# W1 chunks and W2 pairs in turn: both halves of W2 by seven products, with the sums carried by ScalarE

## The chip, the cores and the metric

The kernel runs on one core of one Trainium2 chip. The metric is the device time of one execution in microseconds (us). TensorE (PE) multiplies matrices, VectorE (DVE) and ScalarE (ACT) do the elementwise work, SyncE (SP) issues nearly all loads. PSUM has eight banks, each of which holds one sum of 128 x 512 fp32 values.

## The reference

Two layers over 256 positions of width 2048; the change touches the MLP alone, which stands once in each layer:

```python
def sq_relu_mlp(x, w1, w2):
    return jnp.square(jax.nn.relu(x @ w1)) @ w2        # w1 2048 x 8192, w2 8192 x 2048

for layer in range(2):
    mix = short_conv_mixer(...) if layer == 0 else mla_mixer(...)
    h = layer_norm(ALPHA * h + mix, ...)
    h = layer_norm(ALPHA * h + sq_relu_mlp(h, w1[layer], w2[layer]), ...)
```

## The kernel before

**Two parts for each number.** Every fp32 operand is split into a high part, rounded for the matmul (`hi`, made by ScalarE), and a low part, what is left (`lo`, made by VectorE); `split` does that (lines 120 to 123). A product is three matmuls: high by high, high by low, low by high (`dot`, lines 271 to 275). For W1 the high weights take both parts of x at once, 512 columns wide (`high`, line 201), and the low weights take x's high part, 256 columns (`low`, line 205).

**Weights.** `stream` lists all weights in the order of their use, in units of 128 x 1024 values (512 KB). `prepare` loads a unit into one of five buffers (`raws`) and splits it into one of eight pairs of buffers (`whl`). `take` hands the next units to a product and prepares ahead of it, up to `LOOK` = 5 units. The order of instructions on each engine is fixed when the program is built, by a scheduler that follows the order of the code for the most part; every engine works through its own list in order.

**The MLP.** `mlp` goes over the 8192 hidden columns in eight eighths (`q`). For each it makes eight chunks of 128 hidden columns (`products`, one chunk is 16 high and 16 low matmuls over 16 K tiles, in turn), evacuates each with ScalarE and VectorE (`whole`), applies Relu and Square, and splits the result. Then it multiplies the eighth by its rows of W2. Two chunks of hidden columns, 256 rows of W2, make a pair. The 2048 output columns are four blocks of 512, for two blocks of 128 tokens.

**Seven products.** A pair times two blocks of output columns, for both token blocks, is a 2 x 2 by 2 x 2 product of blocks: eight block products, or seven by Winograd's scheme, for which sums and differences of the blocks are needed. For the hidden values these are S1 to S4 (lines 604 to 607, VectorE); for the weights T1 to T4 (`prepare`, lines 163 to 176, VectorE too, and their splits). Before, the first two of four output blocks go by seven products in the eighths named in `FAST`, 1 to 6 in layer 0 and 1 to 7 in layer 1 (`down_fast`, seven banks at once; `combine` adds them into `acc`). The rest goes block by block with eight (`down`, `down_late`), and VectorE adds every result into `acc`, which is in SBUF.

**Ends.** The first eighth is done against x that is not normalized yet (`mm_wide`), while `normal` normalizes x. In layer 0 the last eighth is interleaved with transposes for the next layer (`to_wide`), in layer 1 with the last norm and the output (`to_out`).

Of the kernel before, what the change touches and what calls it, by code (L numbers as in the profile page):

```python
# [31 lines left out]
LOOK = 5  # L32
# [3 lines left out]
FAST = {0: range(1, NQ - 1), 1: range(1, NQ)}  # L36
FIRST = ((0, 2, 4, 8), (0, 4, 8))
GROUP = 3
# [4 lines left out]
LAG = 16  # L43
# [4 lines left out]
def trunk(ctx: ExitStack, tc: tile.TileContext, xT, vecs, w_in, w_out, w_kv, w_q, w_uk, w_uv,  # L48
# [12 lines left out]
    ROOM = {"a1": 16896, "a2": 16896, "b": 33280, "c": 16384}  # L61
# [8 lines left out]
    def halves(w):  # L70

        lead = len(w.shape) - 2
        return [(w,)] if lead == 0 else [h for i in range(w.shape[0]) for h in halves(w[i])]
# [5 lines left out]

    def mlp_stream(l):  # L80
        out = []
        for q in range(NQ):
            out += halves(w1[l, q * QC:(q + 1) * QC])
            lead = 0
            if q in FAST[l]:
                out += [(w2f[l, q, j, 0], w2f[l, q, j, 1]) for j in range(QC // 2)]
                lead = 2
            out += halves(w2[l, q, lead:])
        return out
# [4 lines left out]
    stream += halves(w_o) + mlp_stream(1)  # L94

    class Banks:


        more, count = None, 0
# [12 lines left out]
        @classmethod  # L112
        def next(cls):
            cls.count += 1
            return cls.more if cls.more is not None and cls.count % 8 >= 4 else pmm

    state = {"split": 0, "next": 0}
# [13 lines left out]
    def load(i, raw, cuts):  # L131

        hi, lo = ready[i] = parts(i)
        for b0, b1 in zip(cuts, cuts[1:]):
            at, cols = slice(b0, b1), slice(P * b0, P * b1)
            nc.sync.dma_start(raw[:, cols], stream[i][0][:, cols])
            yield
            split(hi[:, at, :], lo[:, at, :], tiled(raw[:, cols]))
            yield
# [6 lines left out]
    def prepare(i):  # L146

        if len(stream[i]) == 1:
            raw = load_raw(i, stream[i][0])
            hi, lo = ready[i] = parts(i)  # L150
            split(hi, lo, tiled(raw))
            return
        r1, r2 = (load_raw(f"{i}_{j}", src) for j, src in enumerate(stream[i]))
        out = []

        def finished(r, name):
            hi, lo = parts(name)
            split(hi, lo, tiled(r))
            out.append((hi, lo))

        b22, (b21, b12) = r1[:, BW:], (r2[:, :BW], r2[:, BW:])
        finished(r1, f"{i}_1")
# [4 lines left out]
        finished(t, f"{i}_t")  # L167
        nc.vector.tensor_tensor(b12, b22, t[:, :BW], ALU.subtract)
        finished(r2, f"{i}_2")
        t4 = r1[:, :BW]  # L170
        nc.vector.tensor_tensor(t4, b21, b12, ALU.subtract)
        f = state["fast"].tile([P, 2, BW], F32R, tag="t4", name=f"t4_{i}")
        split(f[:, 0, :], f[:, 1, :], t4)
        b1, t13, b2 = ([[v.rearrange("p b c -> p (b c)")[:, o:o + BW] for v in w] for o in (0, BW)] for w in out)
        ready[i] = {"11": b1[0], "22": b1[1], "21": b2[0], "T2": b2[1], "T1": t13[0], "T3": t13[1],
                    "T4": [f[:, 0, :], f[:, 1, :]]}

    def size(i):

        return 1 if len(stream[i]) == 1 else 3  # L180

    def take(halves=2):

        i = state["next"]
        state["next"] += halves
        ahead = -sum(size(j) for j in range(i, i + halves))
        for j in range(i, len(stream)):
            ahead += size(j)
            if ahead > LOOK:
                break  # L190
            if j >= state["split"]:
                prepare(j)
                state["split"] = j + 1
        return [ready.pop(i + j) for j in range(halves)]
# [12 lines left out]
    def mm_run(wps, x, k0, k1, nk, tiles_first=False, turn=None):  # L207
# [4 lines left out]
        for k, (w, ps) in order:  # L212
            if k == turn:
                low(ps, w, k, x[k], False)
                high(ps, w, k, x[k], False)
                continue
            high(ps, w, k, x[k], k == 0)
            low(ps, w, k, x[k], k == nk - 1)

    def mm_lag(ps, w, x):  # L220

        for k in range(NC + LAG):
            if k < NC:
                high(ps, w, k, x[k], k == 0)
            if k >= LAG:
                low(ps, w, k - LAG, x[k - LAG], k == NC + LAG - 1)

# [25 lines left out]
    def products(n, x, group=0, cuts=(), turn=None, lag=True):  # L253
# [7 lines left out]
        for i in range(group, n):  # L261
            w = take()
            ps = psum("ps_u")
            if lag:
                mm_lag(ps, w, x)
            else:
                mm_run([(w, ps)], x, 0, NC, NC, turn=turn if i == 0 else None)
# [3 lines left out]
    def dot(ps, w, x, first, last):  # L271

        nc.tensor.matmul(ps, x[0], w[0], start=first, stop=False)  # L273
        nc.tensor.matmul(ps, x[0], w[1], start=False, stop=False)  # L274
        nc.tensor.matmul(ps, x[1], w[0], start=False, stop=last)  # L275
# [34 lines left out]

    FACTORS = (("4", "22", "T4"), ("2", "12", "21"), ("3", "S4", "22"), ("1", "11", "11"),
               ("6", "S2", "T2"), ("7", "S3", "T3"), ("5", "S1", "T1"))

    def down_fast(x, forms):

        ps = {p: psum(f"ps_f{p}") for p, _, _ in FACTORS}
        n = len(x) // 2
        for j in range(n):
            b, = take(1)
            a = {"11": held(x[2 * j], 0), "12": held(x[2 * j + 1], 0), "22": held(x[2 * j + 1], 1)}  # L320
            for i in range(4):
                a[f"S{i + 1}"] = [v[:, j, (4 + i) * P:(5 + i) * P] for v in forms]
            for p, l, r in FACTORS:
                dot(ps[p], b[r], a[l], j == 0, j == n - 1)
        return ps
# [191 lines left out]
    state["split"] = 2 * GROUP  # L517
# [32 lines left out]
    def mlp(idx, ln, begin, blocks, fast):  # L550
# [12 lines left out]

        def block(n, t):
            return acc[:, t, n * BW:(n + 1) * BW]

        def put(n, t, ps):
            if q == 0:
                nc.scalar.copy(block(n, t), ps)
                for _ in range(2):  # L570
                    normal()
            else:
                nc.vector.tensor_tensor(block(n, t), block(n, t), ps, ALU.add)

        for q in range(NQ):
            forms = [array(a, F32R, f"h{idx}_{q}_{a}", QC // 2, 8 * P) for a in ("c", "a2")] if q else None
            if q == NQ - 1:
                begin(block)
            if forms is None:
                ht = array("c", F32R, f"h{idx}_{q}", QC, 2 * T)  # L580
                h = [ht[:, k, :] for k in range(QC)]
            else:
                h = [tuple(v[:, k // 2, (k % 2) * T:(k % 2 + 1) * T] for v in forms) for k in range(QC)]

            def hidden(m, ps, evac, *func):
                if forms is None:
                    f = tmp.tile([P, T], F32, tag="fh", name="fh", bufs=3)
                else:
                    if m % 2 == 0:
                        state["pair"] = fast.tile([P, 8 * P], F32, tag="sf", name="sf")  # L590
                    f = state["pair"][:, m % 2 * T:(m % 2 + 1) * T]
                evac(ps, f, *func)
                if not func:
                    nc.scalar.activation(f, f, AF.Relu)  # L594
                nc.scalar.activation(f, f, AF.Square)
                if forms is None:
                    put_split(h[m], f)
                elif m % 2:
                    hi, lo = (v[:, m // 2, :] for v in forms)
                    src, cols = state["pair"], 4 * P  # L600
                    if q in FAST[idx // 2]:
                        cols = 8 * P
                        a11, a21, a12, a22, s1, s2, s3, s4 = (src[:, i * P:(i + 1) * P] for i in range(8))
                        nc.vector.tensor_tensor(s1, a21, a22, ALU.add)
                        nc.vector.tensor_tensor(s3, a21, a11, ALU.subtract)
                        nc.vector.tensor_tensor(s2, s1, a11, ALU.subtract)
                        nc.vector.tensor_tensor(s4, a12, s2, ALU.subtract)
                    split(hi[:, :cols], lo[:, :cols], src[:, :cols])

            if q == 0:  # L610
                for m in range(QC):
                    if m < GROUP:
                        if m == 0:
                            ws = ln.ws if ln.ws else group_of(GROUP)
                            if not ln.ws:
                                mm_wide(ws, ln.xd)
                            ln.finish()
# [6 lines left out]
                    if m > 0:  # L624
                        normal()
# [393 lines left out]
```

## Time and profile before

| | us |
|---|---|
| median of three runs | 2032.91 (2032.8 to 2034.95) |
| the profiled execution | 2034.58 |
| its span, first to last instruction | 2032.5 |
| TensorE busy | 2013.5 (99%) |
| weight loads of TensorE | 1760.0 (87%) |
| VectorE busy | 1654.6 (81%) |
| ScalarE busy | 1181.9 (58%) |
| read from HBM | 381.25 MB, 189 GB/s over the span |

The granted clock of TensorE is 0.996 over the span. A busy time is the time in which the engine has something in work, so operations that overlap at their ends count once; the mean duration of one operation in a group is longer than the distance from its start to the next one's. In the names, PE is TensorE, PEld its weight loads, SPq the queue of SyncE.

### The profile page before, as it was taken

The page shows a single profiled execution, that of the slowest core. Times are in us where ns is not written, and L with a number is a line of the kernel's source. Part 1 is how long each engine was busy: PE and PEld are TensorE (multiplying, and loading weights), DVE is VectorE, ACT ScalarE, POOL GpSimd, SP SyncE. Part 2 cuts the span into 40 slices and gives each one's busy share as a digit, 9 for nine tenths or more (in the row PEclk, how much of TensorE's full clock was granted, in tenths as well). Part 3 has the DMA queues.
Part 4 walks back from the last instruction along what each step waited for, and adds up shares of the span by engine and source line. Part 5 has one row for each costly group of instructions (what it writes and reads, how often), then busy time and mean ns, then how long its engine had stood idle before and what let it go on. Part 6 is the DMA issues. An engine that isn't in the chain of part 4 may idle for free.

```text
span 2032.5 us, 30055 instructions
## 1 busy us (share of the span) xinstructions
PE 2013.5 (99%) x11208; PEld 1760.0 (87%) x11208; DVE 1654.6 (81%) x2494; ACT 1181.9 (58%) x1752; POOL 2.3 (0%) x21
## 2 busy tenths in 40 slices
PE   9999999999999999999999999999999999999997
PEld 7888888988888888888889998898888888888885
DVE  7667667677898988989688888777889898898988
ACT  6444445576565565655556655467656566565652
POOL 0000000000000000000000000000000000000000
PEclk9999999999999999999999999999999999999998
DMA  8666656564746557475754534656475665746644
GB/s 297 204 190 189 191 189 190 166 202 139 254 145 227 181 182 254 145 233 174 230 176 149 176 122 134 199 171 201 137 248 152 221 210 161 250 145 224 206 164 152
DMA packets 108002, 385.31 MB, mean 190 GB/s; under 512 B 11984, under 2 KB 13392, under 8 KB 107856
## 3 DMA queue, kind: packets, MB, share of 16 engines
q1 hardware_dynamic: 107712, 383.13, 58.8%
q8 instruction: 88, 1.44, 0.3%
q14 instruction: 58, 0.48, 0.1%
q10 hardware_dynamic: 144, 0.26, 0.0%
HBM read 381.25 MB, written 2.10 MB: 189 GB/s over the span
## 4 chain that ended last, share of the span: by engine, by line
PE 96%; DVE 2%; DMA 1%; issue 1%; ACT 0%; DVEq 0%; ACTq 0%
PE ps_u L201 32%; PE ps_u L205 17%; PE ps_d L273 7%; PE ps_d L274 7%; PE ps_d L275 7%; PE ps_f L274 4%; PE ps_f L275 4%; PE ps_f L273 4%; PE ps_w L247 1%; PE ps_w L245 1%; PE ps_w L246 1%; PE ps_g L247 1%; PE ps_g L245 1%; PE ps_g L246 1%; DMA raw<-in_w2f_dram 1%
## 5 line engine op out<-in xcount | busy, mean ns | idle before, releaser
L123 DVE TENSOR_TENSOR lo<-raw,hi 128x1024 fp32r<-128x1024 f32 x712 | 856.9, 1221 | 257.7 <-ACT hi L122 179.9
L122 ACT CAST hi<-raw 128x1024 fp32r<-128x1024 f32 x712 | 743.6, 1051 | 486.4 <-PE ps_u L201 268.9
L201 PE MATMUL ps_u<-xhl,hi 128*128 128x512 f32 x1792 | 622.1, 392 | 0.0
L205 PE MATMUL ps_u<-xhl,lo 128*128 128x256 f32 x1792 | 499.6, 280 | 0.0
L201 PEld LDWEIGHTS ps_u<-xhl,hi 128*128 128x128 f32 x1792 | 334.4, 187 | 73.1
L205 PEld LDWEIGHTS ps_u<-xhl,lo 128*128 128x128 f32 x1792 | 338.6, 189 | 1.7
L273 PE MATMUL ps_d<-hi,h_c 128*128 128x512 f32 x480 | 186.8, 389 | 0.0
L275 PE MATMUL ps_d<-hi,h_a 128*128 128x512 f32 x480 | 186.6, 389 | 0.0
L274 PE MATMUL ps_d<-lo,h_c 128*128 128x512 f32 x480 | 186.6, 389 | 0.0
L201 PE MATMUL ps_u<-xhl_a,hi 128*128 128x512 f32 x720 | 171.9, 391 | 0.0
L201 PEld LDWEIGHTS ps_u<-xhl_a,hi 128*128 128x128 f32 x720 | 132.4, 188 | 25.7
L274 PEld LDWEIGHTS ps_d<-lo,h_c 128*128 128x128 f32 x480 | 90.1, 188 | 18.8 <-DVE lo L123 0.2
L275 PEld LDWEIGHTS ps_d<-hi,h_a 128*128 128x128 f32 x480 | 90.1, 188 | 18.7
L273 PEld LDWEIGHTS ps_d<-hi,h_c 128*128 128x128 f32 x480 | 90.1, 188 | 18.6
L205 PEld LDWEIGHTS ps_u<-xhl_a,lo 128*128 128x128 f32 x720 | 92.3, 191 | 3.5
L594 ACT ACTIVATE sf<-sf 128x256 f32<-128x256 f32 x112 | 46.7, 417 | 82.1 <-DVE sf L331 81.9
L205 PE MATMUL ps_u<-xhl_a,lo 128*128 128x256 f32 x720 | 93.4, 283 | 0.0
L122 ACT CAST hi_t<-raw_t 128x1024 fp32r<-128x1024 f32 x52 | 54.6, 1050 | 47.1 <-DVE raw_t L165 32.0
L330 ACT COPY t<-ps_u 128x256 f32<-128x256 f32 x157 | 57.0, 363 | 42.1 <-PE ps_u L205 42.1
L274 PE MATMUL ps_f<-lo,h_c 128*128 128x512 f32 x208 | 81.2, 390 | 0.2 <-DVE lo L123 0.2
L275 PE MATMUL ps_f<-hi,h_a 128*128 128x512 f32 x208 | 81.1, 390 | 0.0
L273 PE MATMUL ps_f<-hi,h_c 128*128 128x512 f32 x208 | 80.7, 389 | 0.0
(235 smaller groups left out, 3290.8 us busy)
## 6 DMA issues: line engine op xcount, KB each, us to landing
raw<-in_w_dram SPq DMA_DIRECT2D x408, 512.0 KB, 4.4
raw<-in_w2f_dram SPq DMA_DIRECT2D x104, 512.0 KB, 3.6
raw<-in_w_in_dram SPq DMA_DIRECT2D x90, 512.0 KB, 4.2
raw<-in_w_out_dram SPq DMA_DIRECT2D x32, 512.0 KB, 4.0
raw<-in_w_o_dram SPq DMA_DIRECT2D x32, 512.0 KB, 4.1
raw<-in_w_kv_dram SPq DMA_DIRECT2D x10, 512.0 KB, 4.2
raw<-in_w_q_dram SPq DMA_DIRECT2D x8, 512.0 KB, 4.4
raw<-in_w_uk_dram SPq DMA_DIRECT2D x8, 512.0 KB, 4.5
```

Source lines behind the costliest of these rows:

```text
L122: nc.scalar.copy(hi, src)
L123: nc.vector.tensor_tensor(lo, src, hi.bitcast(F32), ALU.subtract)
L201: nc.tensor.matmul(ps, w[blk // 8][0][:, blk % 8, :], x, start=first, stop=False)
L205: nc.tensor.matmul(ps[:, :T], w[blk // 8][1][:, blk % 8, :], x[:, :T], start=False, stop=last)
L245: nc.tensor.matmul(ps[:, :W], hi, x[k][:, :W], start=k == 0, stop=False)
L246: nc.tensor.matmul(ps[:, :W], lo, x[k][:, :W], start=False, stop=False)
L247: nc.tensor.matmul(ps[:, :W], hi, x[k][:, W:], start=False, stop=k == NC - 1)
L273: nc.tensor.matmul(ps, x[0], w[0], start=first, stop=False)
L274: nc.tensor.matmul(ps, x[0], w[1], start=False, stop=False)
L275: nc.tensor.matmul(ps, x[1], w[0], start=False, stop=last)
L330: nc.scalar.copy(t, ps[:, T:])
L594: nc.scalar.activation(f, f, AF.Relu)
```

## The change

- A plan (`plan`) replaces the eighths. After the first eighth (eight chunks, as before), one group, which is one pair of K tiles of W2 times one half (two blocks) of the output columns, and one chunk of W1 stand in turn. Pairs 0 to 27 of 32 are done so. The halves take turns: two groups of the first half, four of the second, four of the first, and so on. The first three groups follow each other, and three chunks are left over at the end. There are 56 groups and 56 chunks in each layer.
- In both halves every pair of these goes by seven products but the first two (`PLAIN`, eight products). The last four pairs of W2 go block by block with eight products, in both layers.
- The seven sums stay in seven banks over a run of groups. When the half changes (`turn`), ScalarE copies each sum out to SBUF (`spill`) and the other half's sum back into its bank (`seed`), 14 copies; the matmuls then go on adding. Before the last blocks, VectorE adds up the sums of the second half (`fold`) and those of the first (`combine`). The adds into `acc` after every eighth are gone.
- While the sums hold their banks, chunks of W1 have one bank. A chunk does eight high and then eight low matmuls for each of its two units (`mm_like`). Elsewhere `mm_lag` becomes `mm_like`, in the same order.
- `take` prepares by steps, eight units in all from the one in use on; a group by seven products counts three. T4 and the tiles of the forms have two buffers each. S2 and S3 come from one operation.
- The calls that prepare the next norm are spread over the groups in layer 0 (`prepare_one`); in layer 1 the residual is turned before the last blocks rather than before the last eighth.

The diff, cut to its core:

```diff
-LOOK = 5
 RAW, WA = 5, 8
-FAST = {0: range(1, NQ - 1), 1: range(1, NQ)}
+PAIRS = FF // (2 * P)
+KEPT = PAIRS - QC // 2
+SLOTS = 10
+PLAIN = ((0, 1), (0, 1))
...
+    def plan():
+        nxt, b, steps, m, count = [0, 0], 0, [], QC, 0
+        while min(nxt) < KEPT:
+            end = min(nxt[b] + (4 if nxt != [0, 0] else 2), KEPT)
+            run = [(b, j, j in PLAIN[b]) for j in range(nxt[b], end)]
+            for i, (b, j, plain) in enumerate(run):
+                steps.append(("group", b, j, plain, i == 0, i == len(run) - 1))
+                if count >= 3 and m < FF // P:
+                    steps.append(("m", m))
+                    m += 1
+                count += 1
+            nxt[b], b = end, 1 - b
+        return steps + [("m", i) for i in range(m, FF // P)]
...
     def prepare(i):
...
         t = raws.tile([P, 1024], F32, tag="raw", name=f"raw{i}_t")
         two = "p (a c) -> p a c"
         nc.vector.tensor_tensor(t.rearrange(two, a=2), b12.unsqueeze(1).to_broadcast([P, 2, BW]),
                                 r1.rearrange(two, a=2), ALU.subtract)
-        finished(t, f"{i}_t")
         nc.vector.tensor_tensor(b12, b22, t[:, :BW], ALU.subtract)
-        finished(r2, f"{i}_2")
...
+        out["11"], out["22"] = finished(r1, 1)
+        nc.vector.tensor_tensor(b11, b21, b12, ALU.subtract)
+        yield
+        out["T1"], out["T3"] = finished(t, "t")
+        yield
+        out["21"], out["T2"] = finished(r2, 2)
+        f = state["fast"].tile([P, 2, BW], F32R, tag="t4", name=f"t4_{i}", bufs=2)
+        split(f[:, 0, :], f[:, 1, :], b11)
...
+    def take(n=2):
+        i = state["next"]
+        state["next"] += n
+        while state["made"] < min(start[i] + WA, start[-1]):
+            next(making)
+            state["made"] += 1
...
+    def mm_like(ps, w, x, n=NC):
+        for h in range(0, NC, n):
+            for k in range(h, h + n):
+                high(ps, w, k, x[k], k == 0)
+            for k in range(h, h + n):
+                low(ps, w, k, x[k], k == NC - 1)
...
+    FAST = (("1", "11", "11"), ("3", "S4", "22"), ("7", "S3", "T3"), ("5", "S1", "T1"),
+            ("2", "12", "21"), ("6", "S2", "T2"), ("4", "22", "T4"))
...
+        def spill(self, p):
+            if p in self.live:
+                nc.scalar.copy(self.slot(self.live.pop(p)), self.bank[p])
+
+        def seed(self, p, key):
+            if key in self.store:
+                nc.scalar.copy(self.bank[p], self.at(key))
+                self.drop(key)
+                self.live[p] = key
...
+        def turn(self, b, plain):
+            for p, _, _ in FAST:
+                if p in self.bank:
+                    self.spill(p)
+                    self.seed(p, (b, "C" if p == "1" and plain else p))
...
+        sums = Sums(idx)
+        Banks.only = Banks.more
+        count = 0
+        for at, step in enumerate(steps):
+            if step[0] == "m":
+                m = step[1]
+                w, ps = take(), psum("ps_m")
+                mm_like(ps, w, xhl, 8)
+                if m % 2 == 0:
+                    f = pair()
+                half = f[:, m % 2 * T:(m % 2 + 1) * T]
+                whole(ps, half)
+                if m % 2:
+                    nc.scalar.activation(f[:, :4 * P], f[:, :4 * P], AF.Relu)
+                    square(f)
+                    j, cols = m // 2, 4 * P
+                    if j < KEPT:
+                        forms(f)
+                        cols = 8 * P
+                    split(one[:, j % 4, :cols], two[:, j % 4, :cols], f[:, :cols])
+                if m == FF // P - 3:
+                    Banks.only = None
+                continue
+            _, b, j, plain, first, last = step
+            w, = take(1)
...
+            sums.group(b, w, parts_of(j), plain, last, turns)
+            if later:
+                if last:
+                    sums.turn(later[0][1], later[0][3])
...
+            if first and j + 4 >= KEPT and b == 0 and j + 2 >= KEPT:
+                folded = sums.fold(1)
+            if not later:
+                folded = sums.combine(0) + folded
+            if count < 4:
+                normal()
+                normal()
...
-        combine(put, down_fast(h, forms))
         for n in range(2):
+            down(h, put, n)
             for t in range(2):
                 counted(n, t)
         down_late(h, finished, range(2, NB))
```

More of the change, by code (lines that the diff above doesn't have):

```diff
@@ L42 @@
 COL = 128
-LAG = 16
 C_G, C_B, C_CW, C_QG, C_KG, C_END = 0, 64, 128, 176, 180, 184
@@ L94, in trunk @@
     stream += halves(w_o) + mlp_stream(1)
+    size = {"unit": 1, "plain": 2, "fast": 3}
+    start = [0]
+    for kind, *_ in stream:
+        start.append(start[-1] + size[kind])
     class Banks:
-        more, count = None, 0
+        more, count, only = None, 0, None
         @classmethod
@@ L114, in next @@
             cls.count += 1
+            if cls.only is not None:
+                return cls.only
             return cls.more if cls.more is not None and cls.count % 8 >= 4 else pmm
-    state = {"split": 0, "next": 0}
+    state = {"made": 0, "next": 0}
     ready = {}
@@ L251, in group_of, with products @@
         return [(take(), psum("ps_g")) for _ in range(n)]
-    def products(n, x, group=0, cuts=(), turn=None, lag=True):
+    def products(n, x, group=0, cuts=()):
         ws = group_of(group)
@@ L564, in block @@
         def block(n, t):
[L565 removed]
+            return folded[n][t]
         def put(n, t, ps):
[L568 to L617, printed above, removed]
[L618 to L637 removed]
@@ L639, in combine @@
[L639 to L655 removed]
+            nc.vector.tensor_tensor(block(n, t), block(n, t), ps, ALU.add)
@@ L657, in turned, with to_wide @@
+        h = [(one[:, k // 2, k % 2 * T:(k % 2 + 1) * T], two[:, k // 2, k % 2 * T:(k % 2 + 1) * T]) for k in range(QC)]
+        blocks(block, put, h)
+    def to_wide(block, put, h):
         def turned(n):
```

277 lines of the change are left out of this document (163 added, 114 removed).

## The prediction, made before the changed kernel ran

> **What bounds the kernel now.** I read the page first: busy times, the slices, the chain that ended last.
>
> ```profile
> span 2032.5 us, 30055 instructions
> PE 2013.5 (99%) x11208; PEld 1760.0 (87%) x11208; DVE 1654.6 (81%) x2494; ACT 1181.9 (58%) x1752; POOL 2.3 (0%) x21
> PE   9999999999999999999999999999999999999997
> DVE  7667667677898988989688888777889898898988
> PE 96%; DVE 2%; DMA 1%; issue 1%; ACT 0%; DVEq 0%; ACTq 0%
> ```
>
> TensorE is busy in every slice and makes 96% of the chain. Busy matmuls are not yet matmuls at full rate, so I took start times from the timeline of PE, once inside a W2 block and once in the W1 chunk behind it:
>
> ```profile
> 699.67 0.39 PE L274 MATMUL ps_d<-lo,h_c 128*128 128x512 f32 x1
> 714.17 0.39 PE L275 MATMUL ps_d<-hi,h_a 128*128 128x512 f32 x1
> 714.40 0.39 PE L201 MATMUL ps_u<-xhl,hi 128*128 128x512 f32 x1
> 714.63 0.28 PE L205 MATMUL ps_u<-xhl,lo 128*128 128x256 f32 x1
> 719.97 0.39 PE L201 MATMUL ps_u<-xhl,hi 128*128 128x512 f32 x1
> 27.39 3.67 PE ps_u L201 x16
> 31.06 1.91 PE ps_u L205 x16
> 32.97 3.65 PE ps_u L201 x16
> ```
>
> From 699.67 to 714.17 there are 64 steps of one 128x512 matmul: 0.2266 us each. A W1 chunk of 16 high and 16 low matmuls, alternating, takes 719.97 - 714.40 = 5.57 us. The last three rows are from the chain in order of time, an early stage that does its 16 highs first and then its 16 lows: 32.97 - 27.39 = 5.58 us. The order of highs and lows is worth nothing.
>
> So TensorE issues without holes and its matmul count sets the time. VectorE, which makes every low part, is at 81%, and 8 or 9 tenths in most slices of the MLPs. Its rows, from the timeline:
>
> ```profile
> 560.34 0.28 DVE L604 TENSOR_TENSOR sf<-sf 128x128 f32<-128x128 f32 x1
> 560.66 0.29 DVE L606 TENSOR_TENSOR sf<-sf 128x128 f32<-128x128 f32 x1
> 574.86 0.68 DVE L123 TENSOR_TENSOR t<-raw,t 128x512 fp32r<-128x512 f32 x1
> 575.46 1.22 DVE L165 TENSOR_TENSOR raw_t<-raw,raw 128x1024 f32<-128x1024 f32 x1
> 576.60 1.22 DVE L123 TENSOR_TENSOR lo<-raw,hi 128x1024 fp32r<-128x1024 f32 x1
> 577.73 0.29 DVE L605 TENSOR_TENSOR sf<-sf 128x128 f32<-128x128 f32 x1
> 577.94 0.69 DVE L168 TENSOR_TENSOR raw<-raw,raw_t 128x512 f32<-128x512 f32 x1
> 578.54 1.22 DVE L123 TENSOR_TENSOR lo<-raw,hi 128x1024 fp32r<-128x1024 f32 x1
> 579.68 0.42 DVE L331 TENSOR_TENSOR sf<-ps_u,t 128x256 f32<-128x256 f32 x1
> 580.01 0.69 DVE L171 TENSOR_TENSOR raw<-raw 128x512 f32<-128x512 f32 x1
> ```
>
> Start to start: 1.13 us for 1024 columns (576.60 to 577.73), 0.60 for 512 (577.94 to 578.54), 0.33 for 256, 0.21 for 128. One that reads what the one before wrote starts some 0.1 us later (560.34 to 560.66 instead of 0.21).
>
> **What goes: matmuls.** A pair by seven products takes 21 matmuls instead of 24. Before, 13 eighths x 4 pairs x one half = 52 pair-halves go so; after, 26 pairs x 2 halves x 2 layers = 104. That is 52 x 3 = 156 matmuls of 128x512 fewer (the built order of the changed kernel has 5928 instead of 6084; all other shapes keep their counts). 156 x 0.2266 = **-35.4 us**, all on the path. W2 is still loaded once, so SyncE's queue carries as many transfers.
>
> **What comes: VectorE's share of each step.** After the start, a step is one group (4.76 us on TensorE: 21 x 0.2266) and one W1 chunk (5.57): 10.33 us. VectorE has in it, for the group: t and three low parts of 1024 columns (4 x 1.13), two differences and T4's low part of 512 (3 x 0.60); for the chunk: two low parts (2.27) and the evacuation (0.33); in every second step also the forms and the pair's low part (0.21 + 0.33 + 0.21 + 1.13 = 1.88). Sum 8.92 us, or 10.80 with the pair's part, mean **9.86** of 10.33: 95%. Before, the same work stood against down blocks that ask little of VectorE; now 52 such steps follow each other in each layer. The adds into acc (VectorE, 512 columns) go, and none stands in this ledger.
>
> **The loop through the raw buffers.** A share of 95% is safe only if VectorE need not wait. There are five raw buffers, and a step takes five (r1, r2, t and two of W1). The built addresses show that the next group's r1 takes the buffer that t leaves, so its load is issued when t's low part is done. From there to the next group's t low part, in the built order of VectorE: load, ScalarE's high part, then on VectorE low part of r1, t, evacuation, two differences, low part of t.
>
> ```profile
> raw<-in_w2f_dram SPq DMA_DIRECT2D x104, 512.0 KB, 3.6
> DMA to landing us min/median/max: 3.4/4.1/6.6
> 580.46 1.03 ACT L122 CAST hi_t<-raw_t 128x1024 fp32r<-128x1024 f32 x1
> 581.52 1.23 DVE L123 TENSOR_TENSOR lo_t<-raw_t,hi_t 128x1024 fp32r<-128x1024 f32 x1 [0.83 <-ACT hi_t L122]
> core 0: us, PE busy (x) PEld busy (x) DVE busy (x) ACT busy (x) POOL busy (x), PEclk, DMA share, GB/s
> 564.66:602.45 37.79, 37.79 (x201) 32.55 (x200) 36.21 (x52) 26.02 (x39) 0.00 (x0) 1.00 0.40 124
> ```
>
> A load of this tensor lands after 3.6 us (median, page); all raw loads between 560 and 700 us after 3.4 to 6.6, median 4.1. After the change r1 is issued alone and r2 follows 1.13 us later, between the two cases: I take 3.8. High part 1.05; three hand-overs at 0.03 (580.46 + 1.03 to 581.52) make 0.1; VectorE 1.13 + 1.13 + 0.33 + 0.60 + 0.70 + 1.23 = 5.12. The loop is 10.07 us, and in every second step the pair's low part (1.13) stands inside it: 11.20. Mean **10.63**, 0.30 over TensorE's 10.33. 104 steps: **+31 us**. Bounds: at 3.4 us mean 10.23, TensorE paces, 0; at 4.6, mean 11.43, +114. The last row is a stretch of 37.79 us before the change with four group preparations in it (its columns are named in the row above it): VectorE busy 36.21, 96%, TensorE never idle. 9.86 / 0.96 = 10.3 speaks for the lower half, so I stay well below the middle.
>
> **The turns.** After every four groups ScalarE copies seven sums out of PSUM and seven back, 14 copies:
>
> ```profile
> L646 ACT COPY vu<-ps_f 128x512 f32<-128x512 f32 x13 | 7.6, 587 | 38.2 <-DVE acc L573 38.2
> L122 ACT CAST t<-raw 128x512 fp32r<-128x512 f32 x52 | 32.1, 618 | 4.1 <-DVE raw L171 2.9
> L330 ACT COPY t<-ps_u 128x256 f32<-128x256 f32 x157 | 57.0, 363 | 42.1 <-PE ps_u L205 42.1
> L468 ACT ACTIVATE xres<-nu,vec 128x256 f32<-128x256 f32 x48 | 28.5, 598 | 3.9 <-DVE nu L467 3.5
> L594 ACT ACTIVATE sf<-sf 128x256 f32<-128x256 f32 x112 | 46.7, 417 | 82.1 <-DVE sf L331 81.9
> 597.98 1.05 ACT L122 CAST h_c<-sf 128x1024 fp32r<-128x1024 f32 x1
> 598.93 1.05 ACT L122 CAST hi<-raw 128x1024 fp32r<-128x1024 f32 x1
> ```
>
> Out of PSUM is 0.587 us; into PSUM the trace does not show, between 0.417 (256 columns) and 0.618 (512, SBUF to SBUF); I take 0.59, nearest in size: 8.2 us. The Trainium skill (ScalarE: Activation LUTs, Step-by-step) says that ScalarE reaches PSUM faster than SBUF; by that the seven copies back cost somewhat less, and no row here shows it. Queued with the copies in the built order are ten casts of 1024 columns (0.95 start to start), two of 512, an evacuation, Relu and Square (512 columns, 0.62 by the nearest row): 9.5 + 1.2 + 0.4 + 1.2, some 12 us. So the last sum is back 20.2 us after the first left, while TensorE wants it after 4.08 + 5.57 + 4.08 = 13.7 us. The built order of TensorE pulls 6 matmuls of the group after next (1.4 us) and 13 highs and 8 lows of the chunk between (3.9 us) ahead into this hole; 20.2 - 13.7 - 5.3 = 1.2 us are left. In the same two steps TensorE waits 0.6 us for VectorE by the loop above, which covers that much: **0.6 us a turn**, and 24 full turns make **+14 us**. Bounds: 0 where VectorE's waits cover all; 1.6 a turn, +38, if nothing is covered and each copy takes 0.62. A gain is excluded, since nothing goes that ScalarE did in TensorE's way.
>
> **Edits with little behind them.** While the seven sums hold their banks, W1 has one bank: its evacuation (0.36 and 0.42 us) has the next group's 4.76 us to finish in. Normalization: eight of sixteen now stand beside the first plain groups (4 x 5.44 us), three operations of 256 columns on VectorE (1.0 us) and two of 0.60 on ScalarE each, 8 us and 9.6 us in 21.8; the first switch of halves has no chunk between. The fold and the last combine (16 adds of 0.60) stand beside three chunks. I put them together at +4 (0 to 10, the upper end being half of those 9.6 us in each layer). Highs before lows: 0, as above. The residual's transposes move before the last blocks: the same 32, TensorE does them either way.
>
> **Sum.** The profiled execution took 2034.58 us, 2.1 over its span; the median of the three runs, 2032.91, is 1.7 below it. 2034.6 - 35.4 + 31 + 14 + 4 = 2048.2; as a median **2047 us**. A measurement can tell 0.2% (4 us) from no change.
>
> **Rivals.** (a) *TensorE keeps the pace*: loads land at 3.4 us, VectorE's loop is 10.23, and VectorE catches up at each turn. For it: the 96% stretch, in which TensorE did not wait. Against: there it had stored work and only four groups. 2032.9 - 35.4 + 10 to 24 = 2008 to 2022, say **2015**: faster. It decides at a landing time of 3.5 us. (b) *ScalarE's turns alone*: no raw-buffer wait, but 1.6 us a turn: 2032.9 - 35.4 + 38 + 4 = **2040**. (c) *Transfers jam*: four loads of 512 KB within 5 us of each step land at 4.6 us or later: 2047 + 83 = **2130**; the 6.6 in the row above is for it, the page's 3.6 against. (d) *VectorE's operations do not overlap*: by whole durations (1.22, 0.69, 0.42, 0.29) the ledger is 6.95 for the group, 2.86 for the chunk and 1.11 for half a pair, 10.92 us a step, 0.59 over TensorE (61 us in 104), and with turns and edges 2032.9 - 35.4 + 61 + 18 = **2077**; the start times above (1.13 for 1.22) speak against it. The Trainium skill (VectorE: DVE Perf Modes, The DRAIN you can't avoid) says that the next operation does not start until the pipe has emptied; the trace disagrees for these operations. That the matmuls do not go is excluded by the built order.
>
> **Chances.** Forecast 0.52, (a) 0.27, (b) 0.10, (c) 0.08, (d) 0.03. Faster by over 0.2%: nearly all of (a), and 0.03 of the forecast's low end: 0.29. Within 0.2%: 0.02 of (a), 0.04 of the forecast, 0.03 of (b): 0.09. Slower: 0.62. Range 2008 to 2108: it leaves out some of (a) below, most of (c) and the forecast's upper end above. The forecast alone is 2028 to 2108.
>
> **What would show it.** Right: in the steady steps, low part of r1 waits for its high part and that for the load by 0.5 to 1 us, evacuations lag the chunk by several us, PE has small holes of 0.3 us a step and 0.6 more at each turn, VectorE near 93% over these stretches. Wrong: PE dense between turns (a), holes only where a product waits for a copied sum (b), loads at 4.6 us or more (c).

## The result, and the profile after

The changed kernel takes 2040.74 us (median of seven runs, 2037.91 to 2046.94) against 2032.8 us: ratio 1.0043, 95% interval [1.0032, 1.0054], slower by 7.9 us. The forecast was 2047. The profiled execution took 2046.94 us, 12.4 more than the profiled one of before; it is the longest of the seven, so what is lost in it adds up to some 6 us more than in a median run. Its granted clock is 0.995, that of the median run 0.998.

The page of the changed kernel, its first lines, the chain that ended last, and four groups of instructions (busy us, mean ns of one, idle us before them):

```profile
span 2045.2 us, 29837 instructions
PE 2004.7 (98%) x11052; PEld 1732.7 (85%) x11052; DVE 1761.7 (86%) x2543; ACT 1392.0 (68%) x2071; POOL 2.3 (0%) x21
DVE  7667677799999999989978888879999999999996
PE 54%; DVE 23%; DMA 15%; ACT 7%; issue 2%; DVEq 0%; ACTq 0%; SPq 0%
L145 DVE TENSOR_TENSOR lo<-raw,hi 128x1024 fp32r<-128x1024 f32 x712 | 859.0, 1220 | 161.1 <-ACT hi L144 82.2
L297 PE MATMUL sum<-lo,hc 128*128 128x512 f32 x464 | 185.6, 400 | 12.6 <-DVE lo L145 12.6
L585 ACT COPY sums<-sum 128x512 f32<-128x512 f32 x192 | 111.0, 585 | 4.7 <-PE sum L298 4.0
L589 ACT COPY sum<-sums 128x512 f32<-128x512 f32 x174 | 103.0, 592 | 1.2
```

TensorE has 156 matmuls fewer (11052), and yet the span is longer. Its share of the chain fell from 96% to 54%; what came in are VectorE (23%) and loads (15%). VectorE is at nine tenths through both MLPs.

Where TensorE loses time shows in a table of windows of the changed kernel: two turns (first and third row, from the first copy of a sum to the last) and the stretches behind them, then two later turns.

```profile
core 0: us, PE busy (x) PEld busy (x) DVE busy (x) ACT busy (x) POOL busy (x), PEclk, DMA share, GB/s
538.80:558.50 19.70, 19.26 (x96) 15.88 (x96) 18.67 (x24) 19.28 (x30) 0.00 (x0) 1.00 0.61 189
558.50:581.50 23.00, 23.00 (x121) 19.78 (x120) 21.19 (x26) 14.79 (x21) 0.00 (x0) 1.00 0.61 199
581.50:599.90 18.40, 17.60 (x84) 13.86 (x83) 17.72 (x22) 18.30 (x30) 0.00 (x0) 1.00 0.54 169
599.90:624.40 24.50, 24.50 (x130) 21.09 (x129) 22.66 (x28) 15.73 (x21) 0.00 (x0) 1.00 0.64 216
756.10:777.10 21.00, 18.29 (x81) 14.61 (x80) 18.36 (x24) 19.36 (x29) 0.00 (x0) 0.92 0.53 167
887.50:909.10 21.60, 19.01 (x77) 14.59 (x76) 19.02 (x24) 19.43 (x30) 0.00 (x0) 0.84 0.48 163
```

At a turn ScalarE is busy nearly all the time (19.28 of 19.70 us) and TensorE has holes; between turns TensorE is full and ScalarE at 64%. Summed over the pair stages, with every distance between the starts of two matmuls taken against its nominal 0.2267 us (512 columns) or 0.1197 (256) and those above by 0.03 or more counted, TensorE loses 48.1 us: 47.1 at turns, 1.0 elsewhere. Not all of it is waiting: at three of the 24 turns (the last two rows show two, with 0.92 and 0.84) the granted clock falls to 0.50 for 3.4 or 6.8 us, 13.7 us in all, and matmuls of 512 columns start 0.43 us apart there instead of 0.23; by this some 5 us of the 48.1 are clock (an estimate). So the sum forecast for all stalls (31 + 14 + 4 = 49) is there, but it does not stand where the prediction put it. Read alone, this profile says: ScalarE's copies cost 2 us a turn. What TensorE waited for says something else (us in total, times, longest):

```profile
PE sum L297 <- DVE lo L145: 12.6, 23, 1.3
PE sum L296 <- ACT hi_t L144: 5.4, 6, 1.5
PE sum L296 <- ACT sum L589: 3.7, 7, 1.6
```

These three rows are 21.7 us of the 48.1. Parts of weights that came late make the most of them, a copied sum (L589) the least. In the waits of TensorE's weight loads a copied sum counts for more, 11.9 us against 22.1 and 10.4 for the same two parts, so that this profile alone does not decide. Three theories were therefore put to the test. L: the loop through the raw buffers, as in the prediction, makes the loss, and it only shows at the turns. T: ScalarE's copies make it. V: VectorE's load as such does.

### The profile page after: what moved, and what is told of

It reads as the page before. It is cut to its first block, busy times and chain, and to the rows that moved or that the text cites. A ratio compares the mean times of both kernels' runs of the same rounds, so it can differ in the third digit from the quotient of the medians.

```text
span 2045.2 us, 29837 instructions
## 1 busy us (share of the span) xinstructions
PE 2004.7 (98%) x11052; PEld 1732.7 (85%) x11052; DVE 1761.7 (86%) x2543; ACT 1392.0 (68%) x2071; POOL 2.3 (0%) x21
## 4 chain that ended last, share of the span: by engine, by line
PE 54%; DVE 23%; DMA 15%; ACT 7%; issue 2%; DVEq 0%; ACTq 0%; SPq 0%
DMA raw<-in_w2f_dram 14%; PE ps_u L231 13%; PE ps_u L235 7%; PE ps_m L231 6%; DVE lo L145 6%; DVE raw_t L195 4%; DVE lo_t L145 4%; ACT hi L144 3%; PE ps_m L235 3%; PE sum L297 2%; DVE raw L197 2%; PE sum L298 2%; DVE raw L199 2%; PE sum L296 2%; DVE ha L145 1%
## 5 line engine op out<-in xcount | busy, mean ns | idle before, releaser
L231 PE MATMUL ps_m<-xhl,hi 128*128 128x512 f32 x1792 | 456.3, 393 | 0.7 <-DVE sf L338 0.6
L231 PEld LDWEIGHTS ps_m<-xhl,hi 128*128 128x128 f32 x1792 | 331.2, 190 | 66.9 <-DVE sf L338 2.0
L235 PEld LDWEIGHTS ps_m<-xhl,lo 128*128 128x128 f32 x1792 | 245.4, 190 | 18.1
L235 PE MATMUL ps_m<-xhl,lo 128*128 128x256 f32 x1792 | 251.9, 282 | 0.0
L297 PE MATMUL sum<-lo,hc 128*128 128x512 f32 x464 | 185.6, 400 | 12.6 <-DVE lo L145 12.6
L296 PE MATMUL sum<-hi,hc 128*128 128x512 f32 x464 | 181.6, 397 | 3.2 <-ACT sum L589 1.8
L298 PE MATMUL sum<-hi,ha 128*128 128x512 f32 x400 | 156.9, 392 | 0.0
L195 DVE TENSOR_TENSOR raw_t<-raw,raw 128x1024 f32<-128x1024 f32 x104 | 127.0, 1221 | 23.1 <-DMA raw<-in_w2f_dram 20.3
L145 DVE TENSOR_TENSOR lo_t<-raw_t,hi_t 128x1024 fp32r<-128x1024 f32 x104 | 126.8, 1219 | 2.8 <-ACT hi_t L144 2.8
L297 PEld LDWEIGHTS sum<-lo,hc 128*128 128x128 f32 x464 | 88.0, 190 | 35.3 <-DVE lo L145 22.1
L585 ACT COPY sums<-sum 128x512 f32<-128x512 f32 x192 | 111.0, 585 | 4.7 <-PE sum L298 4.0
L589 ACT COPY sum<-sums 128x512 f32<-128x512 f32 x174 | 103.0, 592 | 1.2
```

What stands on the lines that cost most here:

```text
L145: nc.vector.tensor_tensor(lo, src, hi.bitcast(F32), ALU.subtract)
L195: nc.vector.tensor_tensor(t.rearrange(two, a=2), b12.unsqueeze(1).to_broadcast([P, 2, BW]), r1.rearrange(two, a=2), ALU.subtract)
L231: nc.tensor.matmul(ps, w[blk // 8][0][:, blk % 8, :], x, start=first, stop=False)
L235: nc.tensor.matmul(ps[:, :T], w[blk // 8][1][:, blk % 8, :], x[:, :T], start=False, stop=last)
L296: nc.tensor.matmul(ps, x[0], w[0], start=first, stop=False, skip_group_check=goes_on)
L297: nc.tensor.matmul(ps, x[0], w[1], start=False, stop=False, skip_group_check=goes_on)
```

## The experiments

All times are medians; "before" ran on the same chip, at 2033.1 to 2033.3 us. Differences to the changed kernel (2040.74) are taken to its own runs, beside which "before" took 2032.8.

| run | us | ratio to before, 95% interval |
|---|---|---|
| no copies at 20 of 24 full turns | 2038.30 | 1.0027 [1.0017, 1.0037] |
| six raw buffers, one for T4 | 2007.65 | 0.9877 [0.9862, 0.9891] |
| one buffer for T4 | 2055.61 | 1.0109 [1.0092, 1.0126] |
| two chunks at the turn | 2048.01 | 1.0078 [1.0063, 1.0093] |
| second difference later | 2080.82 | 1.0230 [1.0215, 1.0245] |
| t made twice | 2172.75 | 1.0683 [1.0665, 1.0702] |
| six raw buffers, two for T4 | 2003.92 | 0.9856 [0.9841, 0.9871] |
| the same, no copies | 1999.29 | 0.9832 [0.9817, 0.9846] |
| second difference later, r1's parts first | 2056.70 | 1.0114 [1.0096, 1.0131] |
| r1's parts first | 2042.87 | 1.0047 [1.0030, 1.0063] |

### No copies at the turns

```diff
         def turn(self, b, plain):
+            self.turns = getattr(self, "turns", -1) + 1
+            if 3 <= self.turns <= 12:
+                return
```

> Leaves out the 14 copies at 10 of the 12 full turns of each layer (the second to the eleventh), so sums of both halves run on in the same banks; the matmuls, loads, splits and their order in the code stay. T (ScalarE's copies make the holes, at the turns alone): 20 of 24 turns lose their some 2 us, and the time falls by 36 to 2005 us, with TensorE dense through the pair stage. L (the prediction's split: the loop through the raw buffers loses 0.30 us a step whatever the copies do, and the lead that TensorE has only shows it at the turns): 31 us stay and 12 go, 2029 us, and holes turn up in the steady steps.

The sums of both halves run into each other here, so this kernel no longer computes the MLP.

Measured: 2038.3 us, 2.4 less than with 280 copies more. T falls: ScalarE's busy time went from 1392.0 to 1250.7 us, and the time hardly moved; the runs of the two kernels overlap (2034.5 to 2044.1, and 2037.9 to 2046.9), so even the 2.4 is not clear of nothing. L's 2029 was too low, since the turns gave less than the 12 us it allowed them. The holes did what L says: TensorE still loses 35.7 us, now for the most part in ordinary steps. (These 35.7 and the 48.1 of the changed kernel differ by 12.4 because the profiled executions do, 2034.54 and 2046.94 us: the one is the shortest of its runs, the other the longest.) The largest wait of TensorE in this run is that of a chunk for the one bank of W1, which VectorE is late to evacuate (12.0 us, 19 times):

```profile
PE ps_m L231 <- DVE sf L338: 12.0, 19, 1.8
PE sum L296 <- ACT sum L589: 6.6, 5, 1.9
```

Without the turns the loop can be read in the timeline (start, duration, in brackets the idle time before). First VectorE over one step of this run, then ScalarE, then SyncE's loads of W2:

```profile
701.21 1.22 DVE L145 TENSOR_TENSOR lo_t<-raw_t,hi_t 128x1024 fp32r<-128x1024 f32 x1
702.34 1.22 DVE L145 TENSOR_TENSOR lo<-raw,hi 128x1024 fp32r<-128x1024 f32 x1
...
707.23 1.23 DVE L145 TENSOR_TENSOR lo<-raw,hi 128x1024 fp32r<-128x1024 f32 x1 [0.80 <-ACT hi L144]
708.71 1.22 DVE L195 TENSOR_TENSOR raw_t<-raw,raw 128x1024 f32<-128x1024 f32 x1 [0.25 <-DMA raw<-in_w2f_dram]
709.85 0.42 DVE L338 TENSOR_TENSOR sf<-ps_m,t 128x256 f32<-128x256 f32 x1
710.18 0.68 DVE L197 TENSOR_TENSOR raw<-raw,raw_t 128x512 f32<-128x512 f32 x1
710.90 0.69 DVE L199 TENSOR_TENSOR raw<-raw 128x512 f32<-128x512 f32 x1
711.51 1.22 DVE L145 TENSOR_TENSOR lo_t<-raw_t,hi_t 128x1024 fp32r<-128x1024 f32 x1
...
722.58 1.22 DVE L145 TENSOR_TENSOR lo_t<-raw_t,hi_t 128x1024 fp32r<-128x1024 f32 x1
```

```profile
706.15 1.05 ACT L144 CAST hi<-raw 128x1024 fp32r<-128x1024 f32 x1 [2.06 <-DMA raw<-in_w2f_dram]
```

```profile
702.46 1.46 SPq L165 DMA_DIRECT2D raw<-in_w2f_dram  x2
712.75 1.46 SPq L165 DMA_DIRECT2D raw<-in_w2f_dram  x2
723.83 1.46 SPq L165 DMA_DIRECT2D raw<-in_w2f_dram  x2
```

t's low part ends at 701.21 + 1.22 = 702.43, and r1's load is issued at 702.46; ScalarE and VectorE then wait for it (2.06 and 0.80 us). The next two steps repeat it, at 712.75 and 723.83. From low part to low part of t it is 10.30 us, and 11.07 in the step with a pair's parts; over 44 steps of each layer (from the starts of t's subtraction) the mean is 10.62 and 10.68 us. The prediction had 10.07, 11.20 and 10.63. In the profiled execution of the changed kernel, with all its copies, the same 44 steps have means of 10.97 and 10.78 us. There too, r1's load was issued within 0.1 us of the end of t's low part in all 102 steps in which this can be seen (104 less the first of each layer).

### Six raw buffers, and T4's second buffer

The room for a sixth buffer came first from T4's tile, then from three tables moved to the attention, where they are loaded too. The control has the second of these two edits alone.

```diff
-RAW, WA = 5, 8
+RAW, WA = 6, 8
-        f = state["fast"].tile([P, 2, BW], F32R, tag="t4", name=f"t4_{i}", bufs=2)
+        f = state["fast"].tile([P, 2, BW], F32R, tag="t4", name=f"t4_{i}", bufs=1)
```

> Six raw buffers instead of five; the room comes from T4's tile, one buffer instead of two, which is run by itself too. L: the loop through five buffers is broken, the 31 us go, 2010 us. T (copies alone fill ScalarE at the turns): within 4 us of the run with one T4 buffer. R (at the turns ScalarE falls behind, buffers come free late, and the next pair's load is then waited for): a buffer more covers the load of some 4 us, and about half of the holes go, 2015 to 2025 us.

> One buffer for T4's high and low part instead of two, nothing else: the control of the run with six raw buffers. T, L and R alike: T4 is the last product but one or two of its group and its part is ready 6 us ahead, so 2041 us within 4; above 2050 the second buffer matters.

Measured: 2007.65 us with six raw buffers, against 2055.61 for its control and 2040.74 for the changed kernel. L's 2010 holds; T's "within 4 us" and R's 2015 to 2025 do not. The control missed its expectation: one buffer for T4 costs 14.9 us with five raw buffers. That T4's high part must then wait for the last product of the group before is the likely reason, but it is not shown: in the control's profile, T4's high part waits for a product four times, 4.5 us in all.

```diff
-    cos_t = const.tile([P, T], F32, name="cos_t")
...
     with tc.tile_pool(name="att", bufs=1) as ap:
+        cos_t = ap.tile([P, T], F32, name="cos_t")
...
+        nc.sync.dma_start(cos_t, cosT)
```

> Six raw buffers and two for T4; the room comes from the sine, cosine and mask tables, which are placed and loaded with the attention instead of at the start. L: the run with six raw buffers and one for T4 took 2007.7 us and still lost 8 us in the pair stage; one T4 buffer cost 15 us with five raw buffers, so part of the 8 goes: 2000 to 2007 us, faster than both kernels. If T4's buffer cost only because it sat in the loop through five buffers: 2007 us, no gain.

Measured: 2003.92 us, 1.4% faster than the kernel before, and the fastest whole version here. The first lines of its page, its chain, and the windows of the same times as above:

```profile
span 2003.3 us, 30066 instructions
PE 1987.9 (99%) x11052; PEld 1731.2 (86%) x11052; DVE 1753.4 (88%) x2543; ACT 1395.0 (70%) x2071; POOL 2.3 (0%) x21
PE 91%; DVE 4%; ACT 2%; issue 1%; DMA 1%; DVEq 0%; ACTq 0%
```

```profile
538.80:558.50 19.70, 19.70 (x103) 16.84 (x102) 19.70 (x24) 18.76 (x29) 0.00 (x0) 1.00 0.64 199
558.50:581.50 23.00, 23.00 (x118) 19.60 (x117) 22.76 (x32) 16.39 (x23) 0.00 (x0) 1.00 0.65 214
```

The same operations on every engine, 37 us less. ScalarE is nearly as full as before (18.76 of 19.70 us in the first window) and TensorE has no hole there; VectorE is at 99% in these windows (42.46 of 42.70 us), and the chain is TensorE's again. From the start of the first full turn to that of the last of each layer, the changed kernel (first two rows) and this one compare as follows:

```profile
495.10:977.90 482.80, 468.66 (x2333) 390.44 (x2332) 445.25 (x529) 376.68 (x529) 0.00 (x0) 0.99 0.58 192
1470.50:1939.00 468.50, 459.85 (x2311) 384.76 (x2310) 439.70 (x523) 373.15 (x524) 0.00 (x0) 1.00 0.59 196
494.80:953.70 458.90, 458.24 (x2331) 387.54 (x2330) 444.76 (x539) 378.46 (x531) 0.00 (x0) 1.00 0.66 203
1441.10:1898.50 457.40, 457.40 (x2333) 388.12 (x2333) 442.26 (x530) 378.79 (x531) 0.00 (x0) 1.00 0.66 203
```

VectorE's idle time falls from 66.4 us to 29.3 and its share rises from 93% to 97%, while these stretches shrink by 35.0 us (951.3 to 916.3): what goes is waiting of VectorE. That speaks against V: the same load on VectorE fits.

### Six raw buffers, no copies

> The same as the run with six raw buffers and two for T4, without the 14 copies at 10 of the 12 full turns of each layer (sums of both halves run on in the same banks). With the loop gone, this prices the turns by themselves: by the prediction's 0.6 us a turn, with nothing of VectorE's waits to cover it 1.2 us, 12 to 24 us less in 20 turns; if ScalarE keeps up at the turns, within 3 us of the run with the copies. L expects the lower end or less, since all that TensorE lost with six buffers was 8 us: 1 to 6 us less.

Measured: 1999.29 us, 4.6 less: 0.23 us for each of the 20 turns left out. L's 1 to 6 holds, the 12 to 24 by the prediction's price does not. This is the price of a turn by itself, with the loop gone.

### Two chunks at the turn

```diff
+                full = len(run) == 4 and count >= 6
+                for _ in range(((1, 1, 0, 2)[i] if full else 1) if count >= 3 else 0):
```

> In each run of four groups from the seventh group on, no W1 chunk after the third group and two after the fourth, so that TensorE has 11.1 us of chunks between the last group of a half and the first of the other instead of 5.6. T: the 2 us holes of a turn are covered, less a wait of the second chunk for the one bank that the first one's evacuation must free (it queues behind copies on ScalarE): 2010 to 2025 us. L: the steps need as long on average, 2041 us or more. A new wait of the second chunk for its bank of over 2 us a turn would eat the gain.

Measured: 2048.01 us, 7.3 more. T expected 2010 to 2025. The cover for the copies is doubled and nothing is gained by it, but the wait that the expectation named came too: the second chunk waits for its bank, as the weight loads of a chunk's high parts show (35.0 us for VectorE's evacuation, against 2.0 in the changed kernel):

```profile
L233 PEld LDWEIGHTS ps_m<-xhl,hi 128*128 128x128 f32 x1792 | 323.7, 188 | 96.0 <-DVE sf L340 35.0
```

That is 1.5 us for each of the 24 turns with two chunks, most of the 2 us that T hoped to cover, so this run by itself does not tell T from L.

### What stands in the loop: t made twice, and the second difference later

```diff
         nc.vector.tensor_tensor(t.rearrange(two, a=2), b12.unsqueeze(1).to_broadcast([P, 2, BW]),
                                 r1.rearrange(two, a=2), ALU.subtract)
+        nc.vector.tensor_tensor(t.rearrange(two, a=2), b12.unsqueeze(1).to_broadcast([P, 2, BW]),
+                                r1.rearrange(two, a=2), ALU.subtract)
```

> The subtraction that makes t (128 x 1024, 1.13 us start to start) is done twice into the same place, inside the loop. L: the loop is 10.65 + 1.13 = 11.8 us, 1.45 over TensorE in each of 104 steps, where it was 0.32: 117 us more than the changed kernel, 2158 us; some 10 less where the scheduler puts another operation in the gap. V: the ledger is 9.86 + 1.13 = 11.0 us, 0.66 over TensorE, 69 us in all where some 40 are lost now: 2070 to 2085 us. T (ScalarE at the turns): VectorE's load does not matter below 10.33; above it the same 2070 to 2085.

Measured: 2172.75 us, 132.0 more, for 104 operations of 1.13 us (118 us). L's 117 is the nearest; V and T had 30 to 45. An operation added inside the loop costs about its full time. The 14 us above that need not be the loop's: the granted clock of these runs is 0.980 to 0.984, where the changed kernel has 0.995 to 0.998, which is some 30 us of TensorE's time (an estimate, 0.015 of 2172).

```diff
         out["11"], out["22"] = finished(r1, 1)
-        nc.vector.tensor_tensor(b11, b21, b12, ALU.subtract)
         yield
         out["T1"], out["T3"] = finished(t, "t")
+        nc.vector.tensor_tensor(b11, b21, b12, ALU.subtract)
```

> Five raw buffers as in the changed kernel; the second difference (512 columns, 0.60 to 0.70 us, L199 before) is written behind t's low part instead of ahead of it, so that t's buffer, which the next pair's first load takes, comes free earlier; no operation is added or removed. In the built order it stands behind t's low part in most steps, and in part of them the low part of r1 moves behind t. L (the loop through the five raw buffers paces the steps at 10.62 to 10.68 us, as without the copies): the loop falls to 9.9 to 10.4 us, at or under TensorE's 10.33, and 20 to 30 us of the 33 that a sixth buffer brought come back, 2010 to 2020 us. V (VectorE's load as such, 95% with no room for its jitter, and the sixth buffer only gave room for it): the same operations, 2041 us within 5.

Measured: 2080.82 us, 40 more, where L had 20 to 30 less and V nothing. V is out, since the operations are the same. But L as I had written it fails too. VectorE's timeline of this run shows why:

```profile
707.64 1.23 DVE L195 TENSOR_TENSOR raw_t<-raw,raw 128x1024 f32<-128x1024 f32 x1 [1.13 <-DMA raw<-in_w2f_dram]
708.79 1.22 DVE L145 TENSOR_TENSOR ha<-sf,hc 128x1024 fp32r<-128x1024 f32 x1
709.92 0.69 DVE L197 TENSOR_TENSOR raw<-raw,raw_t 128x512 f32<-128x512 f32 x1
710.52 1.22 DVE L145 TENSOR_TENSOR lo<-raw,hi 128x1024 fp32r<-128x1024 f32 x1
711.66 0.42 DVE L338 TENSOR_TENSOR sf<-ps_m,t 128x256 f32<-128x256 f32 x1
712.00 1.22 DVE L145 TENSOR_TENSOR lo_t<-raw_t,hi_t 128x1024 fp32r<-128x1024 f32 x1
713.13 0.69 DVE L201 TENSOR_TENSOR raw<-raw 128x512 f32<-128x512 f32 x1
713.73 1.22 DVE L145 TENSOR_TENSOR lo<-raw,hi 128x1024 fp32r<-128x1024 f32 x1
```

There is a second loop, through r2's buffer, which r2's own low part frees (713.73 + 1.22 = 714.95; r2's next load is issued at 714.97). The second difference stands ahead of that low part in either order, so nothing was gained. And the scheduler, which had more room, moved the low part of r1 and a pair's low part (`ha`) from ahead of t, where they filled the time in which r2's load was in flight (VectorE now idles 1.13 us there), to behind it, into the loop. In the built order 75 of 104 groups have r1's low part behind t, where the changed kernel has 30, and 27 a pair's low part, where it has 9. With the low parts of chunks, the traces have 75 operations of 1024 columns more than the changed kernel between the start of t and the low part of r2.

The next two runs try this account (O), with r1's parts written ahead of t, once with the difference later and once without:

```diff
+        out["11"], out["22"] = finished(r1, 1)
         t = raws.tile([P, 1024], F32, tag="raw", name=f"raw{i}_t")
...
-        out["11"], out["22"] = finished(r1, 1)
```

> The second difference later, as in the run that came out 40 us slower than the changed kernel, but the parts of r1 written ahead of t. In that run the scheduler had put r1's low part behind t in 75 of 104 groups (30 in the changed kernel) and a pair's low part between t and r2's low part in 27 (9), 75 operations of 1024 columns more between t and the low part of r2 that frees r2's buffer for the next load. Here it is 29 more and 2 fewer. O (what stands between a load's landing and the release of its buffer sets the time, r2's buffer as much as t's): by 40 us for 75 operations, 27 cost 14 us: 2050 to 2060 us. L as I had it (t's buffer alone): the difference is out of the loop in about half the groups, 2025 to 2035. V (VectorE's load alone): 2041.

> The control: the parts of r1 written ahead of t, the second difference where the changed kernel has it. Between t and r2's low part stand 9 operations of 1024 columns more and 8 fewer. O, L and V alike: 2041 us within 5.

Measured: 2056.7 and 2042.87 us. O's 2050 to 2060 holds, and so does the control. Over the changed kernel, 75 operations behind t cost 40.1 us and 27 cost 16.0: 0.53 and 0.59 us each, some of which may be clock (0.992 to 0.996 in the first of these kernels, 0.994 to 0.998 in the second). O's price per operation came from the one run and was tried on the other; why an operation of 1.13 us costs half its time there was not measured.

## Why the prediction was right, and where it was not

**The sum.** From the runs: matmuls -35.4, the loop 2040.7 - 2003.9 = +36.8, the turns 24 x 0.23 = +5.5, the edges at most +0.7 (below), together +7.6; measured 7.9 (2040.74 - 2032.8). These terms are differences of the same runs, so that they add up proves nothing; what they give is the size of each. The forecast 2047 is 6.3 too high, from three terms that are each off: loop +5.8, turns -8.5, edges -3.3. That it came so near owes something to luck, since the first of these offsets half of the other two.

**Matmuls, -35.4: right.** With loop and turns gone the kernel takes 1999.29 us, 33.8 less than before. The 1.6 that are missing hold four full turns (0.9) and the edges, so these are at most 0.7 and not 4: that cover held better than assumed.

**The loop, +31: the mechanism was right, the size 6 us low.** One more buffer takes the loss away. The loop's period without copies is 10.62 to 10.68 us against the forecast 10.63, but that agreement is partly luck. The landing of 3.8 us that I took lies between two cases which both occur in each step of the changed kernel: r1's load 3.63 us (median), r2's, issued 1.13 us later, 4.48. The loop that I had summed goes through r1 alone; with 3.63 its sum is 10.46 on average and the loss 14 us, not 31. In the run without copies (means of the 88 steps) the landing takes 3.63, from there to the start of t 2.88, and from there to the end of t's low part 4.10: the landing is 0.17 shorter than I took it, the rest 0.15 longer. With the copies the period is 10.87 in the profiled execution, 11.3 in steps that a turn covers for more than 5 us and 10.6 in the others: ScalarE's copies stand in the loop as well, and the prediction's two terms are not independent. What the prediction missed is that r2 has a loop of its own, about as long; t reads both, and in 40 of 102 steps of the changed kernel it starts within 0.15 us of r2's landing. So a change that shortens t's loop alone gains nothing, and I forecast the wrong sign for such a change afterwards. The Trainium skill (Perfetto Trace Analysis, Optimization Strategy) says that the same gap, repeated on the engine that should be full, can mean too few buffers for the next tile; the sixth buffer agrees, but here the gaps on TensorE were neither in every step nor equal, and what repeated was VectorE's wait for ScalarE's high parts (33.9 us in 56 waits between the first and the last full turn of the two layers, against 16.8 in 42 with six buffers).

**The turns, +14: too high.** The queue of 20.2 us on ScalarE was sized well (19.28 us busy in 19.70). What failed is the step from there to 0.6 us a turn: TensorE lacks 0.23, with nothing of VectorE's waits left to cover it, where that step gave 1.2. Which of the products that TensorE pulls ahead covers the rest was not followed.

**Where the holes stand: wrong.** The prediction wanted 0.3 us in each step and 0.6 more at a turn; the trace has 1.0 us in all steps together and 47.1 at the turns. It had named a TensorE dense between turns as the sign of rival (a), and holes where a product waits for a copied sum as that of (b). The loss is made in every step and paid at the turn: with the copies gone most of the holes stay (35.7 us, and 48.1 in the longer execution of the changed kernel), and turn up in ordinary steps. That TensorE lives on parts made ahead in between is my reading: in layer 0 of the changed kernel, from the first full turn on, t's low part was ready 4.9 to 8.9 us before its first product. How a turn uses that lead up was not measured.

**The rivals.** (b), ScalarE's turns alone, gave 2040, the measured time to the microsecond, and is wrong: the copies are worth 2.4 us with five buffers (not clear of nothing) and 4.6 with six. (a) asked for loads at 3.4 us, and no more than 3.5; the medians are 3.63 and 4.48. (c) asked for 4.6 us or more, which they do not reach either. (d) is out, as the start times show again (701.21 to 702.34, 1.13 us for an operation of 1.22). The section of the Trainium skill that the prediction names for (d) (VectorE: DVE Perf Modes, The DRAIN you can't avoid) adds that a next operation which is not held starts earlier; with that sentence it does not stand against these start times. By its own parts, the chance of a faster kernel is 0.28, not 0.29.

**The other signs: right.** VectorE was expected near 93%; from the start of the first full turn to that of the last it is at 93.0% (884.95 of 951.3 us). The waits of low parts for their high parts, expected at 0.5 to 1 us, are 0.6 us on average (33.9 us in 56). The evacuation of a chunk on VectorE starts 2.6 us (median) behind the chunk's last matmul.

## What to carry to other kernels

Holes stand where an engine runs out of what was made ahead, and that is not always where the time is lost: leave out what stands at the hole before believing it. Where a load's buffer is freed by an operation that itself needs the load before, add up that loop with everything the scheduler puts inside it, for each buffer by itself; a busy share of 93% can be a loop of waits. One more buffer was worth 37 us here, when its room could be had from tables that were not in use, while a reordering of the same operations cost 40.

## What the runs showed of the hardware that I had not expected

ScalarE's copies of 128 x 512 out of PSUM took 585 ns and those into PSUM 592. The Trainium skill (ScalarE: Activation LUTs, Step-by-step) calls PSUM the faster destination. These two rows differ in their source as well as in their destination and do not test that; the nearest row from SBUF to SBUF, a cast of the same size, took 614, which agrees with it as far as it goes.

Two loads of 512 KB, issued 1.13 us apart on one queue, landed after 3.63 and 4.48 us (medians). Over all 712 weight loads of this size in the changed kernel the median is 3.6 us with no other in flight at the issue, 4.4 with one and 4.6 with two.

In the profiled executions with five raw buffers the granted clock of TensorE fell to 0.50 inside the pair stage in six of eight, in stretches of 3.4 or 6.8 us; in the three with six raw buffers it did not. What sets it off was not tested.
